# A decoder layer with 201 MB of expert weights: x and mem also come transposed, the norm's weights are applied at the split, and token tile 0 ends the projection and routes ahead of tile 1

## The chip, the cores and the metric

The kernel runs on one core of a Trainium2 chip. The metric is the device time of one execution in microseconds; the median of three runs stands for a kernel. A profile is one execution, recorded by the hardware.

## The reference

A decoder layer on 256 tokens of width 1024, all float32:

```
h   = rmsnorm(x) * attn_g ;  m = rmsnorm(mem) * mem_g
GLA (4 heads, chunks of 64, low-rank gate), MoBA (4 heads, causal softmax with ALiBi,
QK-norm), memory attention (4 heads into 256 memory tokens, QK-norm)  from  h @ w_in, m @ w_mem_kv
x2  = x + concat(heads) @ w_out
f   = rmsnorm(x2) * ffn_g
group = argmax(f @ w_rg + b_rg); two experts of the group's eight by f @ w_re + b_re
out = x2 + sum over the two of  p_group * p_e * ( silu(f @ w_gate[e]) * (f @ w_up[e]) ) @ w_down[e]
```

There are 32 experts of three 1024x512 matrices each, 201 MB in all. The kernel reads every expert's weights, whatever the routing.

## The kernel before

**Weights and their buffers.** All weights pass through SBUF in chunks of 1 MB, 128 partitions by 2048 floats. A pool `ring` has RING = 22 such buffers, and SyncE (SP) issues all loads in one order (line 106). First come 16 chunks of the attention part (`w_in`, `w_mem_kv`, `w_out`, packed by the host) and one buffer for mem; then 192 chunks of expert weights, 24 for each of 8 batches of four experts. In a batch, 16 chunks belong to gate and up (`w0g`, `w0u`) and 8 to down (`w0d`). Of every 25 expert chunks, the last three (LATE) lie in a pool that takes over the space of the attention part's scratch. Seven ring buffers hold no weights at first but scratch of the attention part: `hT` (two, the transposed x as a high and a low part), `memT` (two; later `mix`, the heads' output, which the output projection reads) and `sg0`, `sh0`, `sh1`. A load whose buffer is still in use waits on SP, and all loads behind it wait too. Expert chunks are numbered from 0 below: chunk 24 is the last for which there is room before the first expert chunk is used up; chunk 25 needs the buffer of a chunk that the gate product of batch 0 has read.

**Split products.** The projections are computed with two float32r parts per operand: `hi` is a rounded copy and `lo` the rest; `mm` runs three products, hi·hi, lo·hi and hi·lo (PASSES). `w(name, n)` splits one 128x512 piece of a weight chunk: ScalarE makes hi, VectorE makes lo. Before, `w` also multiplies each piece by the norm's weight (`gain`), and `x_T` and `mem_T` transpose x and mem on TensorE in pieces, which ScalarE and VectorE then split into hi and lo. hi has three buffers, lo two. The norm's weights come as rows in 14 small loads; `gains_T` turns them into columns.

**Order.** Inside the attention part every engine runs a list written out by hand (`order`), and `InOrder` keeps each engine to it. In the list `mb` (MoBA's q, k), `qk`, `e` (values of MoBA and mem's q), `kv`, `v`, `r` and `o` are projections; `gate_*`, `decayed` and `states` belong to GLA. The projection by `w_out` (`o`) runs both token tiles side by side, piece by piece, and its halves are added to `x2` (`add`). Then `row_T` transposes x2, `logits` and `bias` make router logits, `choose` picks groups and experts, `place` and `hot` make positions and a one-hot matrix, and `gather0` collects the tokens of the first four experts by products with it. After that the expert batches run (`batch`); gate and up first, then down.

Of the kernel before, what the change touches and what calls it, by code (L numbers as in the profile page):

```python
# [73 lines left out]
def layer(tc, x, mem, attn_norm_g, mem_norm_g, w_in, w_gla_gk, b_gla_gk, gla_out_norm_g,  # L74
          moba_q_norm_g, moba_k_norm_g, w_mem_kv, mem_q_norm_g, mem_k_norm_g, w_out,
          ffn_norm_g, w_router_group, b_router_group, w_router_expert, b_router_expert,
          w_gate, w_up, w_down, attn_pack, moe_pack, out):
    nc = tc.nc
    with ExitStack() as ctx:
        const = ctx.enter_context(tc.tile_pool(name="const", bufs=1))  # L80
        keep = ctx.enter_context(tc.tile_pool(name="keep", bufs=1))
# [45 lines left out]
        for s in [m[:, 0, 0:2] for m in hT + memT]:
            pool.memset(s.bitcast(F32), 0.0)

        win = w_in[0].rearrange("(i p) e -> p i e", p=P)  # L130

        def load_mem(t):
            r = mem_slot[0][:, D * t:D * t + D]
            load(out=r, in_=mem[0, P * t:P * t + P])
            return r


        gain_rows = [sg0[0:8, 1024:1152], sg0[32:47, 1024:1152]]
        gain_cols = fconst.tile([P, 24], F32, name="gain_cols")
        gfn = fconst.tile([P, KD], F32, name="gfn")  # L140
        g_attn, g_mem = (gain_cols[:, 8 * n:8 * n + 8] for n in range(2))
        g_qk, gno, bgk = gain_cols[:, 16:20], gain_cols[:, 20:21], gain_cols[:, 21:23]

        chunks = {}

        def load_chunk(name, h):

            chunks[name, h] = chunk(attn_pack[ATTN_CHUNKS.index((name, h))], f"w_{name}{h}", (4, 512))
# [15 lines left out]
        def load_small(what):  # L164
            rows = gain_rows[1]
            if what == "attn":
                load(out=gain_rows[0], in_=attn_norm_g[0].rearrange("(i p) -> i p", p=P))
            elif what == "mem":
                mem_slot.append(slot("mem"))
                mems.update((t, load_mem(t)) for t in range(NT))  # L170
            elif what == "mem gain":
                load(out=rows[0:8], in_=mem_norm_g[0].rearrange("(i p) -> i p", p=P))
            elif what == "ffn":
                load(out=g_ffn, in_=ffn_norm_g[0].rearrange("(p i) -> p i", i=KD))
                load(out=gfn.rearrange("p (q j) -> p q j", q=2), in_=ffn_norm_g[0].rearrange("(q p j) -> p q j", q=2, j=4))
            elif what == "qk gains":

                for n, g in enumerate((moba_q_norm_g, moba_k_norm_g, mem_q_norm_g, mem_k_norm_g)):
                    for half in range(2):
                        load(out=rows[8 + n:9 + n, 64 * half:64 * half + 64], in_=g[0:1])  # L180
            elif what == "gla":
                load(out=rows[12:13], in_=gla_out_norm_g[0:1])
                load(out=rows[13:15], in_=b_gla_gk[0].rearrange("(n p) -> n p", p=P))
            elif what == "lr":
                load(out=wlr, in_=win[:, :, 1536:1552])
            elif what == "gk":
                for p0 in (0, 32):
                    load(out=wgk[p0:p0 + 16], in_=w_gla_gk[0])
            elif what == "router":
                for q in range(2):  # L190
                    load(out=wr[:, 0, 4 * q:4 * q + 4, 0:4],
                         in_=w_router_group[0].rearrange("(q p j) g -> q p j g", q=2, j=4)[q])
                    load(out=wr[:, 1:5, 4 * q:4 * q + 4].rearrange("p g j e -> p g (j e)"),
                         in_=w_router_expert[0].rearrange("g (q p j) e -> q p g (j e)", q=2, j=4)[q])
                load(out=br[:, 0:4], in_=b_router_group[0:1, :].broadcast_to([P, 4]))
                load(out=br[:, 8:40], in_=b_router_expert.rearrange("l g e -> l (g e)").broadcast_to([P, 32]))

        loads = [
            (load_x, 0), (load_x, 1), (load_small, "attn"), (load_chunk, "mb", 0), (load_small, "mem gain"),
            (load_small, "lr"), (load_chunk, "mb", 1), (load_chunk, "qk", 0), (load_small, "qk gains"),  # L200
            (load_small, "mem"), (load_small, "gk"), (load_chunk, "e", 0), (load_small, "gla"), (load_chunk, "qk", 1),
            (load_chunk, "o", 0), (load_chunk, "e", 1), (load_chunk, "v", 0), (load_chunk, "kv", 1),
            (load_chunk, "r", 0), (load_chunk, "kv", 0), (load_chunk, "v", 1), (load_chunk, "r", 1),
            (load_small, "ffn"), (load_chunk, "o", 2), (load_chunk, "o", 3), (load_chunk, "o", 1),
            (load_small, "router"),
# [150 lines left out]
        def more_constants():  # L356
            state["iota_s"] = iota(const.tile([P, C], F32, name="iota_s"), [[1, C]], base=1)
            state["iota_e"] = iota(const.tile([P, NE], F32, name="iota_e"), [[1, NE]])
            state["iota_g"] = iota(const.tile([P, NE], F32, name="iota_g"), [[1, 4], [0, 8]])
# [5 lines left out]
            state["ones"] = const.tile([P, P], BF16, name="ones")
            pool.memset(state["ones"], 1.0)
            pool.memset(wr[:, 0, :, 4:8], 0.0)
            pool.memset(br[:, 4:8], -BIG)
            pool.memset(cur, 0.0)
# [11 lines left out]
        def w(name, n):  # L381

            src = chunks[name, n // 4][:, n % 4]
            hi, lo = weights[name, n] = [stage.tile([P, 512], F32R, name=f"{name}{n}_{part}", tag=part, bufs=bufs)
                                         for part, bufs in (("hi", 3), ("lo", 2))]
            if name == "o":
                split(src, hi, lo)
            else:
                gain = (g_mem if name == "kv" else g_attn)[:, n:n + 1]
                act.activation(hi, src, AF.Copy, scale=gain)  # L390
                dve.scalar_tensor_tensor(lo, src, gain, hi.bitcast(F32), op0=ALU.mult, op1=ALU.subtract)
# [80 lines left out]
        def x_T(t, q):  # L472
            norm_T(x2[:, t], t, q, hT, f"x{t}")
# [4 lines left out]
        def mem_T(t, q):  # L478
            norm_T(mems[t], t, q, memT, f"m{t}")

        def gains_T(n):
            rows = gain_rows[n]
            p0, k = 32 * n, rows.shape[0]
            pt = bank("tr", f"pt_gain{n}")[:, 0:k]
            pe.transpose(pt, rows, ident[p0:p0 + k, p0:p0 + k])
            act.copy(gain_cols[:, 8 * n:8 * n + k], pt)
# [40 lines left out]
        def lr_split():  # L527
            dve.tensor_tensor(wlr, wlr, g_attn.unsqueeze(2).to_broadcast([P, KD, 16]), op=ALU.mult)
# [655 lines left out]
```

## Time and profile before

| what | value |
|---|---|
| runs | 576.14, 575.94, 577.19 us; median 576.14 |
| profiled execution | 576.38 us, span 574.8 us, granted clock 0.964 |
| TensorE matmul busy | 482.8 us, 84% of the span |
| VectorE, ScalarE, GpSimd busy | 144.3, 111.1, 32.3 us |
| moved by DMA | 222.02 MB, 386 GB/s over the span |
| chain that ended last | DMA 64%, PE 28%, issue 4% |

The page cuts the span into 40 slices of 14.4 us and gives busy shares in tenths. A chain of waits follows the work that ended last back from the end, at each step to what released it. In timelines a row gives the start in us, the duration in us, the engine, the line, the operation, destination and source tiles, and how many instructions were merged. A float32 product shows as two records, a float32r product or a transpose as one. All operations that go through `InOrder` carry line 68.

### The profile page before, as it was taken

To read this page: it belongs to the slowest core of one execution; us is meant where nothing else is said; L and a number is where in the kernel's file an instruction comes from. 1 tells how busy PE (TensorE), PEld (TensorE's weight loads), DVE (VectorE), ACT (ScalarE), POOL (GpSimd) and SP (SyncE) were. 2 spreads that over 40 slices of the span, in tenths; PEclk is the share of its full clock that TensorE was granted. 3 is DMA by queue.
4 is the path that set the end of the run, shared out by engine and by line. 5 is a ranking of instruction groups with operands and counts; after the bars stand their busy time and mean duration, and the time that the engine had idled before them with its cause. 6 is when DMAs were issued, how large, how long until landed. Compare 5 with 4: busy or idle time off the path is not lost.

```text
span 574.8 us, 6813 instructions
## 1 busy us (share of the span) xinstructions
PE 482.8 (84%) x2695; PEld 244.3 (43%) x2695; DVE 144.3 (25%) x316; ACT 111.1 (19%) x217; POOL 32.3 (6%) x72
## 2 busy tenths in 40 slices
PE   5999999999989989777868976698669866996767
PEld 4896777788526226122412521252116211621113
DVE  2769877866306302000100000001000100020002
ACT  5676577642100010000000000001000100010000
POOL 1322230101000000000000000000000000000000
PEclk9999999999998999889997999999889989998899
DMA  8898946698999999999999999999999999999995
GB/s 297 352 421 285 417 151 225 229 391 306 392 421 420 420 423 419 421 421 422 418 421 421 422 418 422 424 418 421 423 422 418 423 421 422 418 423 422 420 421 197
DMA packets 35401, 222.02 MB, mean 386 GB/s; under 512 B 7411, under 2 KB 7974, under 8 KB 8742
## 3 DMA queue, kind: packets, MB, share of 16 engines
q1 hardware_dynamic: 34934, 221.02, 94.1%
q8 instruction: 22, 0.36, 0.3%
q10 hardware_dynamic: 432, 0.52, 0.2%
q14 instruction: 13, 0.11, 0.0%
HBM read 220.49 MB, written 1.05 MB: 385 GB/s over the span
## 4 chain that ended last, share of the span: by engine, by line
DMA 64%; PE 28%; issue 4%; DVE 2%; ACT 1%; POOL 1%; SPq 0%; ACTq 0%; DVEq 0%; POOLq 0%
DMA w4u<-in_moe_pack_dram 7%; DMA w3u<-in_moe_pack_dram 7%; DMA w7u<-in_moe_pack_dram 7%; DMA w6u<-in_moe_pack_dram 7%; DMA w5u<-in_moe_pack_dram 7%; DMA w2u<-in_moe_pack_dram 7%; DMA w4d<-in_moe_pack_dram 4%; DMA w7d<-in_moe_pack_dram 3%; DMA w2d<-in_moe_pack_dram 3%; DMA w6d<-in_moe_pack_dram 3%; DMA w5d<-in_moe_pack_dram 3%; DMA w3d<-in_moe_pack_dram 3%; PE pgate L979 2%; PE p_mb L68 2%; PE pup L979 2%
## 5 line engine op out<-in xcount | busy, mean ns | idle before, releaser
L884 PEld LDWEIGHTS pg_b<-ohs_b,x 128*128 128x128 f32 x224 | 55.3, 334 | 11.5 <-issue 10.1
L894 DVE TENSOR_TENSOR sg_b<-sg_b,pup 128x512 f32<-128x512 f32 x8 | 5.5, 688 | 217.3 <-PE pup L979 217.3
L884 PE MATMUL pg_b<-ohs_b,x 128*128 128x128 f32 x224 | 57.3, 407 | 1.9 <-DVE ohs_b L878 1.1
L893 ACT ACTIVATE sg_b<-pgate 128x512 f32<-128x512 f32 x8 | 4.8, 597 | 187.4 <-PE pgate L979 187.4
L887 DVE TENSOR_TENSOR xg_b<-pg_b,g_ffn 128x512 f32<-128x512 f32 x14 | 9.3, 688 | 111.8 <-PE pdn L992 77.5
L918 PE MATMUL acc<-y_b,sT_b 128*128 128x512 f32 x56 | 27.6, 615 | 4.2 <-ACT y_b L916 4.2
L916 ACT COPY y_b<-pdn 128x512 f32<-128x512 f32 x14 | 8.2, 585 | 113.5 <-PE pdn L992 98.1
L941 POOL TENSOR_TENSOR oh<-oh,gates 128x256 f32<-128x256 f32 x8 | 4.9, 616 | 311.1 <-DVE ohs_b L878 301.1
L68 PE MATMUL p_o<-o_hi,memT 128*128 128x512 f32 x64 | 20.6, 403 | 0.0
L979 PE MATMUL pup<-w5u,xg_b 128*32 128x512 f32 x64 | 14.9, 752 | 6.7 <-DMA w5u<-in_moe_pack_dram 6.7
L979 PE MATMUL pup<-w7u,xg_b 128*32 128x512 f32 x64 | 14.7, 738 | 6.9 <-DMA w7u<-in_moe_pack_dram 6.9
L979 PE MATMUL pgate<-w6g,xg_b 128*32 128x512 f32 x64 | 13.9, 753 | 6.0 <-DMA w6g<-in_moe_pack_dram 6.0
L979 PE MATMUL pgate<-w4g,xg_b 128*32 128x512 f32 x64 | 12.3, 673 | 6.9 <-DMA w4g<-in_moe_pack_dram 6.9
L918 PEld LDWEIGHTS acc<-y_b,sT_b 128*128 128x128 f32 x56 | 9.5, 190 | 18.7 <-ACT y_b L916 12.0
L979 PE MATMUL pup<-w6u,xg_b 128*32 128x512 f32 x64 | 12.9, 637 | 4.5 <-DMA w6u<-in_moe_pack_dram 4.5
L979 PE MATMUL pup<-w2u,xg_b 128*32 128x512 f32 x64 | 12.9, 758 | 4.0 <-DMA w2u<-in_moe_pack_dram 4.0
L979 PE MATMUL pup<-w4u,xg_b 128*32 128x512 f32 x64 | 11.8, 619 | 4.9 <-DMA w4u<-in_moe_pack_dram 4.9
L979 PE MATMUL pup<-w3u,xg_b 128*32 128x512 f32 x64 | 11.2, 612 | 5.3 <-DMA w3u<-in_moe_pack_dram 5.3
L68 PE MATMUL pdn<-w7d,hT_b 128*32 128x256 f32 (+1 forms) x96 | 12.4, 453 | 3.6 <-DMA w7d<-in_moe_pack_dram 2.9
L979 PE MATMUL pgate<-w3g,xg_b 128*32 128x512 f32 x64 | 11.7, 682 | 4.0 <-DMA w3g<-in_moe_pack_dram 4.0
L979 PE MATMUL pgate<-w7g,xg_b 128*32 128x512 f32 x64 | 12.0, 639 | 3.6 <-DMA w7g<-in_moe_pack_dram 3.6
L979 PE MATMUL pgate<-w5g,xg_b 128*32 128x512 f32 x64 | 11.9, 636 | 3.7 <-DMA w5g<-in_moe_pack_dram 3.7
(321 smaller groups left out, 759.2 us busy)
## 6 DMA issues: line engine op xcount, KB each, us to landing
w0g<-in_moe_pack_dram SPq DMA_DIRECT2D x8, 1024.0 KB
w0u<-in_moe_pack_dram SPq DMA_DIRECT2D x8, 1024.0 KB
w0d<-in_moe_pack_dram SPq DMA_DIRECT2D x8, 1024.0 KB
w1g<-in_moe_pack_dram SPq DMA_DIRECT2D x8, 1024.0 KB
w1u<-in_moe_pack_dram SPq DMA_DIRECT2D x8, 1024.0 KB
w1d<-in_moe_pack_dram SPq DMA_DIRECT2D x8, 1024.0 KB
w2g<-in_moe_pack_dram SPq DMA_DIRECT2D x8, 1024.0 KB
w2u<-in_moe_pack_dram SPq DMA_DIRECT2D x8, 1024.0 KB
```

What stands on the lines that cost most here:

```text
L68: r = getattr(self.engine, name)(*args, **kwargs)
L884: nc.tensor.matmul(pgs[q][:, j], x2_i[:, t, 4 * q + j], ohs[:, t], start=(t == 0 and j == 0), stop=(t == NT - 1), skip_group_check=True)
L887: nc.vector.tensor_tensor(xg[:, 4 * q:4 * q + 4], pgs[q], g_ffn[:, 4 * q:4 * q + 4].unsqueeze(2).to_broadcast([P, 4, P]), op=ALU.mult)
L893: nc.scalar.activation(sg, pg, AF.Silu)
L894: nc.vector.tensor_tensor(sg, sg, pu, op=ALU.mult)
L916: nc.scalar.copy(y, pdn)
L918: nc.tensor.matmul(acc[t][half], sT[:, P * t:P * t + P], y, start=first, stop=last, skip_group_check=True)
L941: nc.gpsimd.tensor_tensor(oh, oh, gates[:, :, EB * b:EB * b + EB].unsqueeze(3).to_broadcast([P, NT, EB, C]), op=ALU.mult)
L979: nc.tensor.matmul(ps[s], xg[:, i, s], tiles[(b, kind, c, e // 2)][:, e % 2, ii], start=(i == 0), stop=(i == KD - 1))
```

## The change

- The host also passes x and mem transposed (`t_pack`, loaded in halves of 512 KB to `raw`); the plain x and mem are still loaded. `x_T`, `mem_T` and `gains_T` go. `x_split(k)` and `mem_split(k)` make hi and lo of one 128x256 piece, eight for each, and multiply it by the norm's weight there; `w` only splits. The small inputs come packed in four loads.
- `warm_up` runs 13 products of zeros before the first data is there; `keep_warm` goes. `x_norm` and `mem_norm` move behind the first products that use the transposed data. lo gets three buffers.
- The ring now also holds two `raw` buffers, and `w4` splits a whole chunk of `w_out` into two ring buffers, twice (four buffers).
- At the end of the projection, tile 0's products come before tile 1's, and tile 0's add, norm, logits, choice and positions are put between tile 1's products. `gather0` is cut by token tile: the part of tile 0 comes ahead of `place(1)`.

```diff
-        hT = [slot(f"hT{n}", F32R).rearrange(...) for n in range(2)]
+        raw = [slot(f"raw{n}").rearrange("p (a b) -> p a b", a=KD) for n in range(2)]
+        hT, memT = [[slot(f"{name}{a}", F32R) for a in range(2)] for name in ("hT", "memT")]
...
         loads = [
-            (load_x, 0), (load_x, 1), (load_small, "attn"), (load_chunk, "mb", 0), (load_small, "mem gain"),
-            (load_small, "lr"), (load_chunk, "mb", 1), (load_chunk, "qk", 0), (load_small, "qk gains"),
...
+            (load, gains, gain_pack), (load_T, 0, 0), (load_chunk, "mb", 0, 0), (load_chunk, "mb", 0, 1), (load_T, 0, 1),
+            (load_chunk, "mb", 1), (load, sh1[:, 0:128], lr_pack), (load_chunk, "qk", 0), (load_x, 0), (load_x, 1),
+            (load_chunk, "qk", 1), (load, wgk, gk_pack), (load_chunk, "e", 0), (load_chunk, "e", 1), (load_T, 1, 0),
+            (load_T, 1, 1), (load_mem,), (load_chunk, "kv", 0), (load_chunk, "kv", 1), (load_chunk, "v", 0),
...
+        def T_split(n, k):
+            src, (hi, lo), gain = raw[n][:, k], ((hT, memT)[n][a][:, k] for a in range(2)), (g_attn, g_mem)[n][:, k:k + 1]
+            act.activation(hi, src, AF.Copy, scale=gain)
+            dve.scalar_tensor_tensor(lo, src, gain, hi.bitcast(F32), op0=ALU.mult, op1=ALU.subtract)
...
+        def w4(name, n):
+            parts = [slot(f"{name}{n}_{v}", F32R).rearrange("p (a b) -> p a b", a=4) for v in ("hi", "lo")]
+            for m in range(4):
+                split(chunks[name, n // 4][:, m], *(v[:, m] for v in parts))
+                weights[name, n + m] = [v[:, m] for v in parts]
...
+        def warm_up(n):
+            ps = bank("tr", "warm_up")
+            for _ in range(n):
+                pe.matmul(ps, zeros[:, 0:P], zeros[:, 0:512], start=True, stop=True)
...
+            (w, "o", 15), (mm, "o", 14, 1), (mm, "o", 14, 0), (w4, "o", 0), (mm, "o", 7, 1), (mm, "o", 7, 0),
+            (w4, "o", 8), (mm, "o", 15, 0), (mm, "o", 15, 1), (mm, "o", 0, 0), (mm, "o", 1, 0), (mm, "o", 2, 0),
+            (mm, "o", 3, 0), (add, 0, 0), (mm, "o", 8, 0), (square, 0, 0), (mm, "o", 9, 0), (row_T, 0, 0, 0),
+            (mm, "o", 10, 0), (mm, "o", 11, 0), (add, 0, 1), (mm, "o", 0, 1), (square, 0, 1), (logits, 0, 0),
+            (mm, "o", 1, 1), (rstd, 0), (row_T, 0, 1, 0), (mm, "o", 2, 1), (mm, "o", 3, 1), (add, 1, 0),
+            (logits, 0, 1), (square, 1, 0), (bias, 0), (mm, "o", 8, 1), (c, 0, 3), (mm, "o", 9, 1), (row_T, 1, 0, 0),
+            (c, 0, 3), (mm, "o", 10, 1), (mm, "o", 11, 1), (logits, 1, 0), (add, 1, 1), (c, 0, 3), (square, 1, 1),
+            (row_T, 1, 1, 0), (place, 0), (logits, 1, 1), (rstd, 1), (h, 0, 3), (bias, 1), (gather0, 0, 0, 4),
+            (c, 1, 9), (gather0, 0, 4, 4), (place, 1), (h, 1, 3), (gather0, 1, 0, 2), (gathered0, 0, 2),
+            (gather0, 1, 2, 2), (gathered0, 2, 2),
```

## Rows read from the trace of the kernel before

**Rows 1.** The page, 40 slices: busy tenths of the DMA engines, and GB/s.
```profile
DMA  8898946698999999999999999999999999999995
GB/s 297 352 421 285 417 151 225 229 391 306 392 421 420 420 423 419 421 421 422 418 421 421 422 418 422 424 418 421 423 422 418 423 421 422 418 423 422 420 421 197
```
**Rows 2.** Windows: busy us (instructions) by engine, clock, DMA share, GB/s.
```profile
0.00:150.00 150.00, 142.57 (x807) 113.09 (x808) 104.23 (x238) 89.13 (x177) 27.95 (x65) 1.00 0.81 309
150.00:560.00 410.00, 329.72 (x1817) 126.17 (x1819) 37.00 (x72) 20.60 (x38) 4.31 (x7) 0.95 1.01 421
40.00:50.00 10.00, 9.99 (x59) 7.78 (x58) 8.23 (x11) 8.13 (x13) 2.54 (x2) 1.00 1.02 409
50.00:60.00 10.00, 8.98 (x46) 6.78 (x45) 9.36 (x20) 5.91 (x11) 2.30 (x2) 1.00 0.78 226
```
**Rows 3.** The chain of waits in order of time: start us, us, what.
```profile
32.54 0.44 PE pt_m L68 x4
51.89 0.60 DVE sg L68
52.49 1.39 DVE e_lo L68
58.00 8.47 PE p_kv L68 x36
197.66 19.79 DMA w2u<-in_moe_pack_dram
537.28 19.83 DMA w7d<-in_moe_pack_dram
557.15 4.50 PE pdn L68 x40
```
**Rows 4.** Timeline of SP's issues: chunks 15, 21, 22 and 25.
```profile
116.62 0.33 SPq L106 DMA_DIRECT2D w0u<-in_moe_pack_dram  x1
132.73 0.33 SPq L106 DMA_DIRECT2D w0d<-in_moe_pack_dram  x1
137.81 0.33 SPq L106 DMA_DIRECT2D w0d<-in_moe_pack_dram  x1
146.48 0.33 SPq L106 DMA_DIRECT2D w1g<-in_moe_pack_dram  x1
```
**Rows 5.** Windows of the first loads, columns as in Rows 2.
```profile
2.00:3.00 1.00, 0.00 (x0) 0.00 (x0) 0.00 (x0) 0.20 (x1) 0.55 (x3) 1.00 0.93 332
```
**Rows 6.** Timeline of TensorE: first products, end of the projection, routing, first gate product.
```profile
10.30 1.22 PE L68 MATMUL p_mb<-mb_hi,hT 128*128 128x512 f32 x2 [0.59 <-ACT mb_hi L68]
14.31 1.05 PE L68 MATMUL p_mb<-mb_hi,hT 128*128 128x512 f32 x2
16.19 0.62 PE L68 MATMUL p_mb<-mb_hi,hT 128*128 128x512 f32 x2
24.19 0.40 PE L68 MATMUL p_qk<-hT,qk_hi 128*128 128x256 f32 x2
132.53 0.98 PE L68 MATMUL pl<-wr,xT 128*128 128x40 f32 x8
140.51 4.05 PE L68 MATMUL pg_b<-ohs,x 128*128 128x128 f32 x16
144.53 1.92 PE L979 MATMUL pgate<-w0g,xg_b 128*32 128x512 f32 x16
```
**Rows 7.** Timeline of ScalarE: splits of 512 and work of 256 columns.
```profile
5.37 0.58 ACT L65 CAST hT<-pt_x 128x512 fp32r<-128x512 f32 x1 [3.16 <-PE pt_x L68]
9.53 1.34 ACT L68 ACTIVATE mb_hi<-w_mb,gain_cols 128x512 fp32r<-128x512 f32 x2 [1.72 <-DMA w_mb<-in_attn_pack_dram]
55.56 0.46 ACT L68 ACTIVATE sh<-p_e,r_x 128x256 f32<-128x256 f32 x1
```
**Rows 8.** Timeline of VectorE: the same.
```profile
5.99 0.69 DVE L65 TENSOR_TENSOR hT<-pt_x,hT 128x512 fp32r<-128x512 f32 x1 [5.99 <-ACT hT L65]
59.25 0.48 DVE L68 SCALAR_TENSOR_TENSOR qn_mq<-p_e,r_x,rs_mq 128x256 f32<-128x256 f32 x1 [0.54 <-POOL rs_mq L68]
```

More of the change, by code (lines that the diff above doesn't have):

```diff
@@ L32 @@
 BIG = 1e30
+HI = 3
 RING = 22
@@ L111, in chunk @@
             return v
+        zeros = work.tile([P, 512], F32, name="zeros", tag="w2").bitcast(BF16)
+        dve.memset(zeros, 0.0)
         ident = const.tile([P, P], F32, name="ident")
@@ L126, in layer @@
             pool.memset(s[:, 0:1], 0.0)
[L127 to L148, printed above, removed]
+        gains = const.tile([P, 40], F32, name="gains")
+        g_attn, g_mem, g_ffn, gfn = (gains[:, n:n + 8] for n in (0, 8, 24, 32))
+        g_qk, gno, bgk = gains[:, 16:20], gains[:, 20:21], gains[:, 21:23]
@@ L159, in layer, with load_chunk @@
-        mems, mem_slot = {}, []
+        chunks, mems = {}, {}
+        def load_chunk(name, h, part=None):
+            src = attn_pack[ATTN_CHUNKS.index((name, h))]
+            if part is None:
+                chunks[name, h] = chunk(src, f"w_{name}{h}", (4, 512))
+                return
+            if part == 0:
+                chunks[name, h] = slot(f"w_{name}{h}").rearrange("p (a b) -> p a b", a=4)
+            load(out=chunks[name, h][:, 2 * part:2 * part + 2],
+                 in_=src.rearrange("p (a b) -> p a b", a=4)[:, 2 * part:2 * part + 2])
@@ L161, in load_x, with load_T @@
+        def load_T(n, q):
+            load(out=raw[n][:, 4 * q:4 * q + 4], in_=t_pack[n, q].rearrange("p (a b) -> p a b", a=4))
         def load_x(t):
             load(out=x2[:, t], in_=x[0, P * t:P * t + P])
[L164 to L196, printed above, removed]
@@ L198, in layer, with load_mem @@
-        loads = [
-            (load_x, 0), (load_x, 1), (load_small, "attn"), (load_chunk, "mb", 0), (load_small, "mem gain"),
-            (load_small, "lr"), (load_chunk, "mb", 1), (load_chunk, "qk", 0), (load_small, "qk gains"),
[L201 to L205, printed above, removed]
+        def load_mem():
+            m = slot("mem").rearrange("p (a b) -> p a b", a=NT)
+            for t in range(NT):
+                mems[t] = m[:, t]
+                load(out=mems[t], in_=mem[0, P * t:P * t + P])
@@ L381, in w @@
         def w(name, n):
[L383 to L391, printed above, removed]
+            hi, lo = (stage.tile([P, 512], F32R, name=f"{name}{n}_{v}", tag=v, bufs=HI) for v in ("hi", "lo"))
+            split(chunks[name, n // 4][:, n % 4], hi, lo)
+            weights[name, n] = hi, lo
+        def w4(name, n):
[3 more added lines that the diff above has]
+                weights[name, n + m] = [v[:, m] for v in parts]
         def sums(name, n):
@@ L470, in x_norm, with x_split, mem_split @@
             norm(x2[:, t], r_x[:, t:t + 1], f"x{t}")
-        def x_T(t, q):
-            norm_T(x2[:, t], t, q, hT, f"x{t}")
+        def x_split(k):
+            T_split(0, k)
         def mem_norm(t):
             norm(mems[t], r_mem[:, t:t + 1], f"m{t}")
[L478 to L486, printed above, removed]
+        def mem_split(k):
+            T_split(1, k)
         def rx_T(part):
@@ L789, in layer @@
         sel = sm_tile([P, NT, NE], "sel", BF16)
-        pps = [bank("at", f"pp{t}")[:, 0:32] for t in range(NT)]
+        pps, pgs0 = {}, {}
         oh0 = oh_pool.tile([P, NT, EB, C], F32, name="oh0", tag="oh")
         ohs0 = oh_pool.tile([P, NT, EB, C], F32, name="ohs0", tag="ohs", bufs=1)
-        xg0 = keep.tile([P, KD, P], F32, name="xg_b0", tag="xg")
         def choose(t):
@@ L826, in gather0, with gathered0, c @@
+        def gathered0(i0, n):
+            dve.tensor_tensor(state["xg0"][:, i0:i0 + n], pgs0[i0 // 4][:, i0 % 4:i0 % 4 + n],
                               g_ffn[:, i0:i0 + n].unsqueeze(2).to_broadcast([P, n, P]), op=ALU.mult)
-        def keep_warm(n):
-            ps = bank("mm", "warm")[:, 0:256]
+        choosing = [choose(t) for t in range(NT)]
+        placing = [hot(t) for t in range(NT)]
+        def c(t, n=1):
             for _ in range(n):
-                pe.matmul(ps, ident, x2[:, 0, 0:256], start=True, stop=True)
@@ L834, in layer, with h @@
-        c0, c1 = (choose(t) for t in range(NT))
-        h0, h1 = (hot(t) for t in range(NT))
-        def steps(*parts):
-            for p in parts:
-                next(p)
-        steps(*[c0] * 3)
-        bias(1)
-        steps(*[c0, c1] * 6)
-        keep_warm(4)
-        place(0)
-        steps(c1, h0, c1, h0, c1, h0)
-        keep_warm(2)
-        place(1)
-        steps(h1, h1, h1)
-        gather0(0, 2)
-        gather0(2, 2)
+                next(choosing[t])
+        def h(t, n=1):
+            for _ in range(n):
+                next(placing[t])
@@ L853, in layer @@
+        for f, *args in order:
+            f(*args)
+        iota_s, iota_e, iota_g, ltri, ones = (state[k] for k in ("iota_s", "iota_e", "iota_g", "ltri", "ones"))
+        fctx.close()
+        ex = ctx.enter_context(tc.tile_pool(name="ex", bufs=2))
+        late = ctx.enter_context(tc.tile_pool(name="late", bufs=LATE))
         ng = sm_tile([P, NT, 2], "ng")
```

205 lines of the change are left out of this document (102 added, 103 removed).

## The prediction

> **What bounds the kernel now.** I read the page's slices first. From about 150 us on the DMA engines never rest: nine tenths in every slice, 418 to 424 GB/s [rows 1]. The window from 150 to 560 us confirms it, 421 GB/s at a share of 1.01, while before 150 us the share is 0.81 [rows 2]. The chain of waits then shows what late time consists of: from 197.66 us it runs from landing to landing, eight chunks in 19.8 us, 2.48 us per chunk of 1 MB, up to 557.1, and only then does TensorE's last work follow [rows 3]. So behind some moment the time is chunks times 2.48 us plus a fixed end, and nothing that TensorE gains there counts. What counts is when that unbroken stream begins.
>
> The timeline of SP's issues gives that moment. Chunk 22 goes out at 137.81, and chunk 25 only at 146.48 [rows 4], when the first gate product (144.53, sixteen records in 1.9 us) has released a buffer [rows 6]. All 25 buffers were full by then; the queue was empty. So before, the stream begins at 146.48, and TensorE's progress sets it. In front of that the DMA engines idled 0.19 x 150 = 28 us for want of free buffers, and TensorE was dense: 142.6 us busy of 150 [rows 2].
>
> **The change part by part.** I call S the number of us by which the projection phase on TensorE comes earlier.
>
> *Start, 5.9 us gained.* Before, the first split product starts at 10.30, after x (1 MB), a 1 MB chunk, transposes and splits; the last of the 48 `mb` products ends by 24.19 [rows 6]. After, x's first half and half a chunk, 1.07 MB, suffice. From 2.0 us at 332 GB/s [rows 5] that is 5.2, with 0.8 us until a wait sees it 6.0; one split of 0.67 (half of the pair at 9.53) [rows 7] gives 6.7. Before, twelve products starting at 10.30 take 4.9 us, 0.41 each: the pair at 14.31 is 1.05 long, that at 16.19 only 0.62, and later ones come every 0.23 us (36 in 8.47) [rows 3, 6]. [...] I take it that the 13 products of zeros, at 0.41 each 5.3 us from about 1.5, bring the rise forward; if not, 12 x 0.2 = 2.4 us are lost again. So 48 x 0.23 = 11.0, plus 0.6 of waiting for the first low halves: 18.3 against 24.19.
>
> *Transposes, 1.3 us gained.* After 24.19 three `mem_T` of 0.44 us go [rows 3].
>
> *A stall, up to 2.0 us gained.* At 51.89 TensorE waits 2.0 us for VectorE, for `decayed` and a low half behind it [rows 3]. With three low buffers VectorE may run ahead. Dense, TensorE would be 5.9 + 1.3 + 2.0 = 9.2 us earlier: the upper bound of S.
>
> *What the splits cost, 2.9 us lost.* They lie in VectorE's fullest stretch. From 40 to 60 us it is busy 8.23 + 9.36 = 17.6 us [rows 2]. Two `mem_T` parts of 0.69 go, eight `mem_split` parts come; the nearest row of 256 columns is 0.48 [rows 8]: 17.6 - 1.4 + 3.8 = 20.0. TensorE could do its own work there in 20 - 0.9 (transposes) - 2.0 (stall) = 17.1. VectorE is then the bound, 2.9 us longer. Between no loss and this I take the full 2.9, since VectorE runs a fixed list and cannot reorder. S = 9.2 - 2.9 = 6.3. ScalarE gets 8 x 0.46 - 2 x 0.58 = 2.5 us more there [rows 7], plus `mem_norm`, on 14.0 busy of 20 [rows 2]: hidden.
>
> The same piece of work tells how the change of shape is priced. Eight of 256 columns cost 8 x 0.48 = 3.8 against 4 x 0.69 = 2.8 us of VectorE per input, 8 x 0.46 = 3.7 against 4 x 0.58 = 2.3 of ScalarE [rows 7, 8]. [...]
>
> *`x_norm` moved behind `qk`'s first products.* `mb_norm` waits for it and `w("qk", 3)` is queued behind both on ScalarE. I price it at nothing, since `mem_norm`, as long, leaves the same stretch; without that cover it is one to two us of S.
>
> *More bytes, nothing.* 2.1 MB more are 5.0 us of DMA at 421 GB/s [rows 2]. They lie before 55 us, ahead of 28 us of DMA idleness. If the cover went, 5.0 us would be paid. The 14 small loads, and SP's waits around them, go at the same place: no effect for the same reason, and all attention chunks come before their use.
>
> *The end of the projection.* Before, tile 1's last product ends at 132.5 [rows 6]. Now two `logits` of 0.98 and a `row_T` of 0.44 stand ahead of it: 132.5 + 2.6 - S. Behind it: `logits` (0.98), `row_T` (0.44) and its copy, `logits`, then gathering tile 0, eight float32 products. Sixteen records, eight products, take 4.05 us [rows 6], so this is 4.05; `place(1)` is queued behind it on TensorE, though it needs none of it. Then one-hot work and two products: about 10.3 us in all. The first gate product starts at 135.1 - 6.3 + 10.3 = 139.1 instead of 144.53.
>
> *Who is late next: the loads.* Before, 24 ring buffers were asked for ahead of chunk 0. Now it is 26 (two `raw` more) and four by `w4`. The two `raw` come back early, so chunk k waits for a release four places later: chunk 11, not 15, gets `sh1`, free at 116.62 before [rows 4]. In my count SP never waits long from there on: 11 to 25 are 15 chunks, each 2.48 us. Chunk 25 is served as if issued 14 x 2.48 = 34.7 after 116.62 - S, at 151.3 - S, against 146.48: a gain of S - 4.9. If `w4` takes buffers only when it runs, four chunks come earlier; but chunk 19 needs `mix` or a `w4` buffer, free at the projection's end (as chunk 21 got `mix` at 132.73 before [rows 4]), so at 135.1 - S, and six chunks on that is 150.0 - S: a gain of S - 3.6 at most. With S = 6.3 these are 1.4 and 2.7; I take 2.0. The gate's 5.4 us are therefore mostly not passed on, because chunk 25 is no longer released by the gate but waits in the queue.
>
> The sum: 576.38 (span 574.8 and 1.6 around it) - 2.0 = 574.4. That execution was 0.24 above the median, so against 576.14 I say 574.3.
>
> **Rivals.** *TensorE keeps everything.* VectorE keeps pace, S = 9.2: gain 4.3 to 5.6, about 571.2. For it: VectorE idles 2.4 us of 40 to 60 and gets a buffer more. Against it: 20.0 us of work for a stretch of 17.1.
>
> *The gain ends at the buffers or is not made.* S is 4 to 5: products of zeros don't raise the clock (S = 3.9), or `x_norm` adds two us. Then -0.3 to +1.0: 576.2. For it: the stream's condition takes 3.6 to 4.9 us of any S.
>
> *Slower: `w4` is served ahead of the loads.* If buffers are given in the program's order, and `w4`'s only when ScalarE reaches it, SP holds chunk 0 until then, two us of splits behind `sh1`'s release: 116.6 + 2.0 - 6.3 = 112.3. Then 25 chunks begin there: chunk 25 is served at 112.3 + 25 x 2.48 = 174.3, against 146.48: 28 us more, 604. It decides at the first expert load: later than 100 us or not. Against it: before, chunks were issued as attention buffers came free.
>
> **How the numbers follow.** Forecast (573.0 to 575.5) 0.50; everything kept 0.15; no gain (575.5 to 577.6, a tenth of it faster) 0.30; `w4` ahead 0.05. A measurement of this kernel tells 0.2% from nothing, 1.15 us: faster is below 575.0. Of the forecast 0.44 lies there, with 0.15 and 0.03: faster 0.62. Same 0.23: 0.06 of the forecast, 0.17 of no gain. Slower 0.15: 0.10 of no gain, and 0.05. The range goes from S = 9.2 with the later bound, 570.6, to S = 3.9 with the earlier, 577.4.
>
> **What would show it.** Right: `mb` ends near 18.3; TensorE waits for VectorE's low halves before `kv`; the gate product starts near 139; SP's issues from chunk 15 on come ahead of the landings by a queue, and chunk 25's buffer is free before its turn. Wrong: DMA idle after 125 us, the first 12 products still 0.41 apart, or a first expert load after 100 us.

## The result, and the profile after

The changed kernel takes 580.66 us (median; 579.87 to 582.46) against 576.14 beside it: ratio 1.0082, 95% interval 1.0057 to 1.0107. It is slower by 4.5 us where 1.8 less were forecast, and above the forecast's upper end of 577.4. The profiled execution has a span of 579.1 us, before 574.8.

The page's slices of the changed kernel, DMA engines and GB/s: nine tenths in every slice from about 116 us on, where before it was from about 144 us on [rows 1]. The stream begins earlier and still ends later.

```profile
DMA  8999537499999999999999999999999999999995
GB/s 296 405 421 386 195 134 278 178 418 407 422 416 420 420 418 419 419 418 420 420 420 421 418 422 417 423 418 418 420 419 421 419 421 418 422 418 421 419 419 200
```

Windows of the changed kernel, columns as in [rows 2]: the first five answer to [rows 2, 5], two more are places where the stream is not full, and in the last the first gate product runs.

```profile
0.00:150.00 150.00, 141.83 (x780) 108.14 (x780) 101.82 (x245) 86.15 (x184) 28.62 (x62) 0.98 0.80 316
150.00:560.00 410.00, 319.44 (x1783) 122.69 (x1780) 37.12 (x72) 21.20 (x38) 4.32 (x7) 0.97 1.01 419
40.00:50.00 10.00, 8.84 (x46) 6.30 (x45) 9.64 (x16) 7.89 (x15) 2.99 (x2) 1.00 1.00 413
50.00:60.00 10.00, 9.08 (x41) 6.65 (x42) 6.58 (x20) 7.99 (x21) 5.29 (x6) 1.00 0.90 348
2.00:3.00 1.00, 1.00 (x4) 0.39 (x3) 0.00 (x0) 0.00 (x0) 0.94 (x3) 1.00 0.57 127
114.00:115.00 1.00, 1.00 (x6) 0.82 (x5) 0.45 (x2) 1.00 (x3) 0.00 (x0) 1.00 0.38 148
130.00:132.00 2.00, 2.00 (x12) 1.72 (x11) 0.68 (x5) 0.59 (x1) 0.00 (x0) 1.00 0.96 336
144.00:146.00 2.00, 2.00 (x12) 0.39 (x8) 0.84 (x6) 1.09 (x6) 0.00 (x0) 0.50 0.99 410
```

The stream moves 419 GB/s and not 421, and VectorE is busy 9.64 of the ten us from 40 to 50, where it was 8.23. From 40 to 60 it is busy 16.2 us in all, not the forecast 20.0: three of the eight `mem_split` parts start before 40.

The chain of waits of the changed kernel: start us, us, what; the stage after `kv`, and rows that answer to the end of [rows 3].

```profile
63.82 1.09 PE pa L69 x16
200.83 19.88 DMA w2u<-in_moe_pack_dram
541.50 19.89 DMA w7d<-in_moe_pack_dram
561.43 4.50 PE pdn L69 x40
```

The last landing in the chain (chunk 187; the other four are not waited for in it) is at 541.50 + 19.89 = 561.39; before it was 557.11 [rows 3]. These 4.28 us are the whole loss of the profiled execution. At the chunk where both chains can be laid side by side (200.83 and 197.66) it is already 3.17; the other 1.1 come later, for a step over eight chunks, pauses aside, takes 19.87 to 19.90 us and not 19.79 to 19.83.

SP's issues of chunks 11 and 25 in the changed kernel, against chunks 15 and 25 of [rows 4].

```profile
113.87 0.33 SPq L106 DMA_DIRECT2D w0u<-in_moe_pack_dram  x1
147.11 0.33 SPq L106 DMA_DIRECT2D w1g<-in_moe_pack_dram  x1
```

Chunk 11 now gets the release that chunk 15 got: the shift by four is as forecast. But that release (`sh1`) comes at 113.87 against 116.62. So S is 2.75 us, and not 6.3. The stage after `kv` shows the same, 63.82 against 66.69 in the chain of the kernel before:

```profile
66.69 1.09 PE pa L68 x16
```

TensorE in the changed kernel: first product, last of `mb`, first of `qk`, three waits, the logits behind the projection, first gate product [rows 6].

```profile
8.46 0.71 PE L69 MATMUL p_mb<-mb_hi,hT 128*128 128x512 f32 x2 [1.32 <-ACT mb_hi L69]
19.70 0.39 PE L69 MATMUL p_mb<-mb_lo,hT 128*128 128x512 f32 x1
19.93 0.40 PE L69 MATMUL p_qk<-hT,qk_hi 128*128 128x256 f32 x2
25.27 0.39 PE L69 MATMUL p_qk<-hT,qk_lo 128*128 128x256 f32 x1 [0.70 <-DVE qk_lo L69]
49.85 0.50 PE L69 MATMUL p_e<-e_lo,hT 128*128 128x512 f32 x1 [0.99 <-DVE e_lo L69]
57.88 0.50 PE L69 MATMUL p_kv<-kv_lo,memT 128*128 128x512 f32 x1 [0.92 <-DVE kv_lo L69]
132.12 0.98 PE L69 MATMUL pl<-wrb,xT 128*128 128x40 f32 x8
143.65 3.42 PE L939 MATMUL pgate<-w0g,xg_b 128*32 128x512 f32 x16
```

All three waits are for low halves, which VectorE writes. The gate product starts 0.9 us earlier, not 5.4, and ends later, for it takes 3.42 us and not 1.92: the granted clock was 0.50 there (from 144 to 146 us). With the old end it takes 1.92 or 1.93 in the runs below.

ScalarE at the start: the first split waits for `raw`, then for its table, then the weights' half lands. The last row is the first of `x_norm`'s two squares.

```profile
4.86 1.28 ACT L66 ACT_TABLE_LOAD   x1 [4.86 <-DMA raw<-in_t_pack_dram]
6.15 0.51 ACT L66 ACTIVATE hT<-raw,gains 128x256 fp32r<-128x256 f32 x1
7.70 0.62 ACT L69 CAST mb_hi<-w_mb 128x512 fp32r<-128x512 f32 x1 [1.04 <-DMA w_mb<-in_attn_pack_dram]
20.42 1.05 ACT L69 ACTIVATE junk_x<-x 128x1024 bf16<-128x1024 f32 x1
```

VectorE in the changed kernel: a split of `mem` between others in `e`, and a wait for GpSimd that holds `kv_lo` back.

```profile
49.72 0.47 DVE L69 SCALAR_TENSOR_TENSOR memT<-raw,gains,memT 128x256 fp32r<-128x256 f32 x1
56.69 0.48 DVE L69 SCALAR_TENSOR_TENSOR qn_mq<-p_e,r_x,rs_mq 128x256 f32<-128x256 f32 x1 [2.38 <-POOL rs_mq L69]
```

### The profile page after: what moved, and what is told of

Its sections match the earlier page's. It is cut to its first block, busy times and chain, and to the rows that moved or that the text cites. A ratio compares the mean times of both kernels' runs of the same rounds, so it can differ in the third digit from the quotient of the medians.

```text
span 579.1 us, 6693 instructions
## 1 busy us (share of the span) xinstructions
PE 474.7 (82%) x2662; PEld 236.9 (41%) x2662; DVE 142.0 (25%) x323; ACT 108.7 (19%) x224; POOL 32.9 (6%) x69
## 3 DMA queue, kind: packets, MB, share of 16 engines
HBM read 222.62 MB, written 1.05 MB: 386 GB/s over the span
## 4 chain that ended last, share of the span: by engine, by line
DMA 76%; PE 19%; DVE 2%; ACT 1%; POOL 1%; issue 1%; SPq 0%; DVEq 0%; POOLq 0%; ACTq 0%
DMA w4u<-in_moe_pack_dram 7%; DMA w3u<-in_moe_pack_dram 7%; DMA w5u<-in_moe_pack_dram 7%; DMA w6u<-in_moe_pack_dram 7%; DMA w2u<-in_moe_pack_dram 7%; DMA w7u<-in_moe_pack_dram 7%; PE p_o L69 4%; DMA w6d<-in_moe_pack_dram 3%; DMA w5d<-in_moe_pack_dram 3%; DMA w7d<-in_moe_pack_dram 3%; DMA w1d<-in_moe_pack_dram 3%; DMA w1u<-in_moe_pack_dram 3%; DMA w3d<-in_moe_pack_dram 3%; DMA w2d<-in_moe_pack_dram 3%; DMA w4d<-in_moe_pack_dram 3%; DMA w_r<-in_attn_pack_dram 3%
## 5 line engine op out<-in xcount | busy, mean ns | idle before, releaser
L844 PEld LDWEIGHTS pg_b<-ohs_b,x 128*128 128x128 f32 x224 | 55.3, 334 | 11.7 <-issue 10.3
L847 DVE TENSOR_TENSOR xg_b<-pg_b,gains 128x512 f32<-128x512 f32 x14 | 9.3, 688 | 110.6 <-PE pdn L953 74.7
L939 PE MATMUL pup<-w4u,xg_b 128*32 128x512 f32 x64 | 13.1, 685 | 6.1 <-DMA w4u<-in_moe_pack_dram 6.1
L939 PE MATMUL pup<-w3u,xg_b 128*32 128x512 f32 x64 | 12.5, 685 | 6.1 <-DMA w3u<-in_moe_pack_dram 6.1
L939 PE MATMUL pup<-w7u,xg_b 128*32 128x512 f32 x64 | 11.6, 600 | 6.1 <-DMA w7u<-in_moe_pack_dram 6.1
L939 PE MATMUL pup<-w5u,xg_b 128*32 128x512 f32 x64 | 11.9, 611 | 5.1 <-DMA w5u<-in_moe_pack_dram 5.1
L939 PE MATMUL pgate<-w7g,xg_b 128*32 128x512 f32 x64 | 10.8, 600 | 6.1 <-DMA w7g<-in_moe_pack_dram 6.1
L939 PE MATMUL pgate<-w6g,xg_b 128*32 128x512 f32 x64 | 10.8, 600 | 6.1 <-DMA w6g<-in_moe_pack_dram 6.1
L939 PE MATMUL pgate<-w4g,xg_b 128*32 128x512 f32 x64 | 10.8, 600 | 6.1 <-DMA w4g<-in_moe_pack_dram 6.1
L953 PE MATMUL pdn<-w2d,hT_b 128*32 128x512 f32 x64 | 10.8, 601 | 5.8 <-DMA w2d<-in_moe_pack_dram 5.8
L939 PE MATMUL pup<-w1u,xg_b 128*32 128x512 f32 x64 | 11.6, 689 | 2.7 <-DVE tmp L1028 2.7
```

The source lines that it names most:

```text
L844: nc.tensor.matmul(pgs[q][:, j], x2_i[:, t, 4 * q + j], ohs[:, t], start=(t == 0 and j == 0), stop=(t == NT - 1), skip_group_check=True)
L847: nc.vector.tensor_tensor(xg[:, 4 * q:4 * q + 4], pgs[q], g_ffn[:, 4 * q:4 * q + 4].unsqueeze(2).to_broadcast([P, 4, P]), op=ALU.mult)
L939: nc.tensor.matmul(ps[s], xg[:, i, s], tiles[(b, kind, c, e // 2)][:, e % 2, ii], start=(i == 0), stop=(i == KD - 1))
L953: nc.tensor.matmul(pdn[half][s], hT2[:, c, s], tiles[(b, "d", c, e // 2)][:, e % 2, 512 * half:512 * half + 512], start=(c == 0), stop=(c ...
```

## The experiments

My theory after this reading: the four buffers of `w4` cost 4.9 us of stream, S gives back only 2.75 since VectorE has no room, and something slows the stream itself. Rivals: the new front as such costs; the gate product still sets the stream. A time below is a median; "before" was 576.3 to 576.7 beside these runs.

### Where the gain went: four runs

**Front alone.** The changed front, with the end of the kernel before.

```diff
-(w4,"o",0) ... (w4,"o",8) ... tile 0's logits, choosing, placing, gathering, then tile 1's
+(w,"o",0) ... both tiles side by side; then steps(...), place, gather0 as before
```

> The changed front (transposed inputs from the host, gains at the split, zeros ahead, third low buffer) with the end of the kernel before: no w4, the two token tiles side by side, routing and gathering in the old order. Theory (queue): the four w4 buffers moved chunk 25's release four places back, so that the stream hangs on the release of sh1 and not on the gate product; without them the stream begins at the gate product again, which comes earlier by what the front gains, 2.8 us: 576.1 - 2.8 = 573.3, and SP issues chunk 25 near 143.7. Rival (front): the 2.1 MB more and the new tensors are what costs, the stream's pace is lower by them: 578 or more, and chunk 15 is again issued at sh1's release. If the slower pace of the changed kernel's stream (19.95 against 19.87 us per eight chunks, 1.3 us over all) belongs to the front, 574.6.

Measured: 576.17 us, ratio 0.9995 (0.998 to 1.001). Neither number. Its SP timeline and its chain of waits:

```profile
115.39 0.33 SPq L106 DMA_DIRECT2D w0u<-in_moe_pack_dram  x1
145.28 0.33 SPq L106 DMA_DIRECT2D w1g<-in_moe_pack_dram  x1
```

```profile
398.77 19.88 DMA w5u<-in_moe_pack_dram
```

Without `w4` it is chunk 15 again that gets `sh1`, and chunk 25 goes out ahead of 146.48 [rows 4] with the gate product: the loss of 4.5 us goes away with `w4`. The step stays at 19.88, so the slower pace belongs to the front, which makes 574.6 of the expected 573.3. The other 1.6 us are not explained. The profiled execution, at 579.27 the slowest of twelve, began at the lower clock (its window from 9 to 12 us, columns as in [rows 2], clock 0.50); whether the other eleven did is not on record.

```profile
9.00:12.00 3.00, 3.00 (x8) 2.16 (x7) 2.99 (x7) 2.76 (x6) 0.00 (x0) 0.50 1.01 419
```

**End alone.** The kernel before with `w4`, the new order behind it and its pools.

> The kernel before with the changed end alone: w4 in four ring buffers, tile 0 projected, routed and gathered ahead of tile 1. Theory (queue): S is 0 here, and the shift costs its full price, 4.9 us of stream and up to 1 us for the stretch behind sh1's release in which the stream is not yet full: 576.1 + 4.9 to 5.9 = 581.0 to 582.0; chunk 11 is issued when chunk 15 was (116.6), although the gate product comes earlier than at 144.5. Rival (front): the end as such is free, its earlier gate product keeps its gain: 576 or less.

Measured: 582.85 us, ratio 1.0114 (1.009 to 1.0138): 6.5 us slower, a little over the upper end. Chunk 11 gets `sh1`; the step is the old one.

```profile
115.92 0.33 SPq L108 DMA_DIRECT2D w0u<-in_moe_pack_dram  x1
```

```profile
395.27 19.81 DMA w5g<-in_moe_pack_dram
```

**A later gate product,** in the changed kernel and in the one before.

```diff
+for _ in range(7): pe.matmul(ps, ident, x2[:, 0, 0:256], ...)   # ahead of place(1)
```

> The changed kernel with seven products of ident and x2 (256 columns, float32, some 3 us) put on TensorE ahead of place(1), so that the first gate product comes 3 us later. Theory (queue): chunk 25's buffer is released about 6 us ahead of its turn, so the time is the same within 0.5 us: 580.7. Rival (gate): the first gate product's release still sets when the stream begins: 583.7.

> The kernel before with seven more products in its keep_warm ahead of place(1), some 3 us. Both theories: here the gate product's release sets the stream, so all of it shows: 579.1, and SP issues chunk 25 near 149.5. If it shows less than 2 us, the reading of the kernel before was wrong: its stream does not hang on the gate product.

Measured: 581.45 (ratio 1.0092, 1.0071 to 1.0113) and 579.03 (1.005, 1.0033 to 1.0068). SP's issue of chunk 25, first in the changed kernel with the delay, then in the one before with it:

```profile
150.56 0.33 SPq L106 DMA_DIRECT2D w1g<-in_moe_pack_dram  x1
```

```profile
149.00 0.33 SPq L106 DMA_DIRECT2D w1g<-in_moe_pack_dram  x1
```

Before, 2.5 us later at the issue gives 2.7 in the time: the gate sets the stream. After, 3.45 us later give 0.8 in the median: it does not. But the spare time was 2 to 3 us and not 6, for with the delay the stream does run dry, as two windows of that kernel show (GB/s last). From issue to landing is longer than a share of the stream: the first two expert chunks of the changed kernel, issued at 54.99 and 58.99, landed after 5.3 and 4.8 us, where a share is 2.48. By an estimate from these, chunk 25 has to be issued the difference, 2.3 to 2.8 us, ahead of its turn to keep the stream whole. The two windows:

```profile
150.00:152.00 2.00, 2.00 (x14) 0.44 (x6) 1.41 (x7) 0.00 (x0) 0.62 (x1) 0.82 0.62 176
152.00:154.00 2.00, 2.00 (x10) 0.66 (x10) 0.43 (x1) 1.12 (x2) 0.00 (x0) 1.00 0.85 340
```

### What slows the stream: five runs

**Old places of the inputs in memory.**

```diff
+for name in _OLD: held[name] = nc.dram_tensor(...)   # all 22 inputs, in the old order
```

> The changed kernel with every input of the kernel before declared again in its old place and order (those not used are never read), so that the packed expert weights lie in memory where they lay before; the instructions are the same. In the runs so far the step between two landings eight chunks apart is 19.88 to 19.90 us in all three kernels with the changed front and 19.79 to 19.82 in all three with the old one, whatever the end. Theory (place in DRAM): the step falls to 19.81, and over the 165 chunks from chunk 23 on, 20.6 steps, the time falls by 20.6 x 0.08 = 1.7 us: 579.0. Rival (something else of the front, as the address of the ring in SBUF, 128 bytes further on): the step stays at 19.89, time 580.7.

Measured: 581.57, ratio 1.0087 (1.0071 to 1.0103). That theory falls, the chain of waits has the same step:

```profile
381.41 19.89 DMA w5u<-in_moe_pack_dram
```

**Start of the ring buffers in SBUF.** The new `gains` tile is 128 bytes longer than the `g_ffn` it replaced and lies ahead of the ring.

```diff
-gains = const.tile([P, 40], ...)
+gains = fconst.tile([P, 40], ...);  g_ffn = const.tile([P, KD], ...)
```

> The changed kernel with the tile gains in the pool that is freed after the projection, and only the eight columns that live on in the constants, as before. So the 22 ring buffers start at byte 19360 of a partition, 416 over a multiple of 512, as in all three kernels with the step of 19.81 (15264 and 19360); in all that showed 19.89 they start at 19488, 32 over. Old places of the inputs in memory did not change the step. Theory (address of the buffers): the step falls to 19.81 and the time by 20.6 x 0.08 = 1.7: 579.0. Rival (nothing of the address): 19.89 and 580.7.

Measured: 579.69, ratio 1.0061 (1.0038 to 1.0084). The chain of waits:

```profile
380.18 19.80 DMA w5u<-in_moe_pack_dram
```

The step is back, and the chain's last landing comes 1.66 us earlier (559.73). The 128 bytes are the cause of the slower step. In the median 1.0 us of the 1.7 shows, and the intervals of the two ratios overlap.

**Ring on a multiple of 512 bytes,** in the version with early norms (below) and in the kernel before; and 256 over.

```diff
+pre = tile_pool("pre")    # iota_s, iota_e, iota_g: 384 bytes (or iota_s alone: 128)
+ring = tile_pool("ring")  # then const, keep, ...
```

> The kernel with the norms early and the old end (575.5), its ring allocated first, behind 384 bytes of constants, so that each buffer starts at a multiple of 512 bytes. Theory (address): a buffer of 8192 bytes that starts on the boundary is served at least as fast as one at 416: step 19.81 or less, time 575.5 - 1.7 = 573.8 or less. Rival: the step stays 19.89 and the time 575.5.

> The kernel before, only its ring allocated first behind 384 bytes of constants (start 1536, a multiple of 512, against 15264). Theory (place alone): the step falls from 19.81 to about 19.55, and the time by 20.6 x 0.26 = 5.4: 570.7. Rival (the place matters only with the changed front): 576.1.

> The same with the ring behind 128 bytes of constants: start 1280, 256 over a multiple of 512. If what counts is the boundary of 512 bytes, the step stays at 19.8 or more (576); if a boundary of 256 does, it is 19.55 as on the multiple (570.7). If the low end of SBUF is what counts, it is 19.55 here too; the step of the kernel before with the ring at 15264 and of the end alone at 19360 were the same, which speaks against that.

Measured: 569.09 (ratio 0.9861, 0.9843 to 0.9879), where the same kernel had 575.47 with its ring 32 over; 571.79 (0.9915, 0.9901 to 0.9928); 572.23 (0.992, 0.9908 to 0.9933). A step of each from the chain of waits, in that order:

```profile
414.08 19.55 DMA w5d<-in_moe_pack_dram
```

```profile
434.89 19.58 DMA w6u<-in_moe_pack_dram
```

```profile
413.96 19.56 DMA w5d<-in_moe_pack_dram
```

So the place alone does it, without the changed front too, and 256 is as good as 512: about 19.56 us at 0 and 256, 19.81 at 416, 19.89 at 32. One rival is left by the edits: all three rings also begin at the low end of SBUF (1280 or 1536, against 15264 to 19488). The chain of the second speaks against it. Its ring begins 15264 - 1536 = 13728 bytes lower, less than two of its 22 buffers of 8192 bytes, and yet all its steps of eight chunks, two pauses aside, take 19.48 to 19.71 us, also those in which no buffer below the old start is filled.

### What held S down: five runs

**Norms early,** with the changed end, and with the old one.

```diff
-(mm,"qk",2,0), (x_norm,1), (mm,"qk",2,1), (x_norm,0) ... (mm,"kv",0,0), (mem_norm,0) ... (mem_norm,1)
+(w,"qk",2), (x_norm,1), (w,"qk",1), (x_norm,0), (w,"qk",0) ... (w,"qk",6), (mem_norm,0), (mem_norm,1)
```

> The changed kernel with three pieces of its order moved: x_norm of both tiles between the first qk weights, where ScalarE waits for TensorE anyway (17.7 to 19.9), both mem_norm behind the seventh qk weight (ScalarE idle 28.1 to 30.8), and mem loaded two loads earlier so that it is there. Theory: the waits at 24.2 to 25.3 (1.0 us, qk_lo behind x_norm) and at 56.9 and 60.3 (1.4 us, kv_lo behind mem_norm's chain over GpSimd) go; S grows from 2.75 to about 5.2, sh1 is released at 111.4, and as the queue starts there all of it reaches the end: 580.7 - 2.4 = 578.3. Rival (VectorE has no room): the gain in qk is eaten where VectorE is late in e, S grows by 1.4 at most and the time is 579.3 or more. Rival (gate): the time follows the gate product, not sh1's release.

> The changed front with the same three moves and the end of the kernel before (no w4). Theory: the stream starts at the gate product, which comes earlier by S: front alone gave 576.2, so 576.2 - 2.4 = 573.8. Rival (VectorE has no room): 574.8 or more.

Measured: 582.99 (ratio 1.0119, 1.0105 to 1.0134) and 575.47 (0.9989, 0.9975 to 1.0003): no gain beyond the noise in either, the rival's side. The first one's release of `sh1` and its wait in `e`:

```profile
113.81 0.33 SPq L106 DMA_DIRECT2D w0u<-in_moe_pack_dram  x1
```

```profile
51.16 0.50 PE L69 MATMUL p_e<-e_lo,hT 128*128 128x512 f32 x1 [1.72 <-DVE e_lo L69]
```

The waits in `qk` and `kv` are gone; the one in `e` grew from 0.99 to 1.72, and `sh1` came 0.06 us earlier; from the first `qk` product (20.25) to it are 93.56 us, in the changed kernel 93.94. In the second one's windows, VectorE (third number with a count) has not a gap:

```profile
44.00:48.00 4.00, 4.00 (x23) 2.89 (x21) 4.00 (x8) 3.25 (x7) 1.61 (x1) 1.00 1.01 412
48.00:52.00 4.00, 2.27 (x13) 1.58 (x12) 4.00 (x8) 1.17 (x3) 1.29 (x1) 1.00 1.02 414
```

Why the first is even slower than the changed kernel stays open. In the profiled execution TensorE's last work begins at 561.15, 0.28 us ahead of the changed kernel's 561.43, so the difference lies behind the stream: that work begins with 6.03 us where it was 4.50.

```profile
561.15 6.03 PE pdn L69 x40
```

**Without the low halves of `mem`** (left out of the computation; norms early, old end).

```diff
-dve.scalar_tensor_tensor(lo, src, gain, hi, ...)   # for mem only
```

> The kernel with the norms early and the old end (575.5), without the eight VectorE instructions that write the low halves of mem (they are zeros here, written once by GpSimd; the output is therefore less exact). Theory (VectorE has no room): it was 4.00 of 4.00 us busy from 44 to 52 and TensorE waited 1.7 us for e_lo at 50.9; with 8 x 0.48 = 3.8 us less that wait goes, S grows by 1.7 to 2.4 and the time falls to 573.1 to 573.8. Rival (the wait is ScalarE's or GpSimd's): S and the time stay.

Measured: 574.12, ratio 0.9954 (0.9938 to 0.997), 0.35% below the kernel with them by the two ratios. TensorE's wait in `e` is 0.35 us. The profiled execution began at the lower clock (0.65 from 9 to 12 us), its first `qk` product came at 21.74 against 19.99 with the low halves, and yet `sh1` was free at 113.60 against 113.58: the stretch between is 1.7 us shorter.

```profile
51.04 0.50 PE L69 MATMUL p_e<-e_lo,hT 128*128 128x512 f32 x1 [0.35 <-DVE e_lo L69]
```

**Splits of `mem` early,** nothing left out.

```diff
-(mem_split,0..7) between the splits of e;  loads: e1, T(1,0), T(1,1), mem
+(w,"qk",6), (mem_split,0..3) ... 4..7 where 0..3 were;  (w,"e",6), (mem_norm,0), (mem_norm,1);  loads: T(1,0), T(1,1), e1, mem
```

> Nothing left out: changed front and old end, x_norm early, mem's first four splits in VectorE's and ScalarE's idle time from 28 to 31 us (mem's transposed halves loaded ahead of the second e chunk), the other four where the first four were, both mem_norm behind the last e weight, and the ring's old address. Theory: VectorE has 1.9 us less in 44 to 52, and the waits in qk and kv go too: S grows from 2.8 to about 5, and the stream starts at the gate product: 575.5 - 2.0 - 1.7 (step 19.81) = 571.8. Rival (VectorE's work is only moved, and comes late elsewhere): 573.8.

Measured: 571.52, ratio 0.9909 (0.989 to 0.9928), as the theory says. The first gate product:

```profile
139.94 1.93 PE L949 MATMUL pgate<-w0g,xg_b 128*32 128x512 f32 x16
```

**Without the products of zeros.**

```diff
-(warm_up, 13),
```

> The changed kernel without the 13 products of zeros. The prediction's term: the first 12 products at 0.40 and not 0.23 us, 2.0 to 2.4 us of S lost at the end of mb. The starts at the lower clock seen in other runs cost 1.5 us of sh1's release (115.05 against 113.58), the rest being eaten by VectorE's stretch: 580.7 + 1.5 = 582.2. Rival (the zeros do nothing): 580.7.

Measured: 584.11, ratio 1.0136 (1.0122 to 1.0151), 3.4 us over the changed kernel and more than expected. In its TensorE timeline the pair that took 0.63 takes 1.05, and `mb` ends 2.2 us later:

```profile
10.04 1.05 PE L69 MATMUL p_mb<-mb_hi,hT 128*128 128x512 f32 x2
21.91 0.40 PE L69 MATMUL p_mb<-mb_lo,hT 128*128 128x512 f32 x1
```

`sh1` is released at 116.08 there, 2.2 us later as well: VectorE's stretch ate nothing of it. The other 1.2 us are not explained.

### All together: two runs

The first is norms early and old end with the old places in memory; the second is splits early with the ring at 1536. Both have

```diff
-(warm_up, 13)
+(warm_up, 20)
```

> The run before, with the old places of the inputs in memory as well and 20 products of zeros in place of 13, so that no gap lies between them and the first real product (in the profiled run of front alone the gap was 2.2 us and the first products came at 0.40 us each and not 0.23). Theory: 573.8 - 1.7 (the step back at 19.81) - about 0.6 (no run starts at the lower clock) = 571.5, and the runs scatter less. If the place in memory is not what slows the step: 573.2.

Measured: 575.59, ratio 0.9985 (0.9972 to 0.9998): a miss, since the memory layout did nothing (above) and 20 zeros for 13 did not move the median.

> The version with the splits early (571.5), its ring at a multiple of 512 bytes and 20 products of zeros in place of 13. The causes add: 571.5 - 20.6 x 0.26 (5.4) - about 0.6 (no start at the lower clock) = 565.5. If they don't add (the faster stream waits for TensorE): 568.

Measured: 566.27, ratio 0.9818 (0.9805 to 0.983): faster than both kernels, 0.8 us from the sum of the parts. Its release of `sh1`, its gate product and a step of its chain, one view each:

```profile
110.72 0.33 SPq L107 DMA_DIRECT2D w0u<-in_moe_pack_dram  x1
```

```profile
138.58 1.92 PE L948 MATMUL pgate<-w0g,xg_b 128*32 128x512 f32 x16
```

```profile
409.32 19.56 DMA w5d<-in_moe_pack_dram
```

S is 116.62 - 110.72 = 5.9 here, near the forecast 6.3, with the same front and its splits and norms in other places.

## Why the prediction was wrong, step by step

**Right: the mechanism.** The stream sets the time, chunk k takes the release of chunk k+4, and of the gate's lead nothing counts any more. Chunk 11's issue shows the shift, the late gate shows the rest, and the end alone is slower where the front alone is not. The first expert load came at 54.99 us, so `w4` was not served ahead of the loads. The 2.1 MB more cost nothing that any run shows. With the measured S the formula S - 4.9 is a loss of 2.15 us. The projection's end also came where its sum puts it with that S: 135.1 - 2.75 = 132.35, and the logits behind it start at 132.12. The gate product then came 1.0 us later than the 10.3 us of routing allow, and took 1.5 longer; neither counted.

**Wrong: the size of S,** a term of the sum: 2.75 and not 6.3. Its start and its stall were taken too large, and the moved norms, priced at nothing, cost time. Up to the end of `kv` the terms were

- the start 4.26 (first `qk` product at 19.93 against 24.19), not 5.9. The weights' half landed at 7.70 and not 6.0: the first loads moved 127 GB/s from 2 to 3 us, where I had taken the 332 of [rows 5]. Zeros were worth 2.2 of it, by the run without them; that they would bring the quicker pace forward was an assumption until then. No run shows the 0.8 us until a wait sees a landing, an estimate of mine: the half landed 5.8 us after its issue at 1.84, and its split began within 0.1 us;
- the stall in `e` 1.0, not 2.0. I took the length of VectorE's links in the chain [rows 3] for TensorE's idle time; the window says 10 - 8.98 = 1.02 [rows 2];
- the transposes 1.3, as forecast, if the three `mem_T` are taken at their 0.44;
- the waits for low halves 2.8 of idle time (0.70 in `qk`, 0.17 and 0.99 in `e`, 0.92 in `kv`), against 2.9. That these are so near is luck, for only the 1.2 in `e` has the forecast cause, a VectorE without room. In `qk` the low half comes late because `x_norm`'s two squares keep ScalarE from 20.42 to 22.5 and `mb_norm` stands behind them; in `kv` VectorE itself idles 2.38 us for GpSimd, where a part of `mem_norm` is ahead in the queue;
- a rest: 4.26 + 1.3 + 1.0 - 2.8 = 3.8, but the stage after `kv` starts 2.9 us earlier (63.82 against 66.69). Most of these 0.9 us lie in `kv`, whose products take 0.8 longer from start to start with no idle time on record; to which term they belong stays open.

So pricing `x_norm` and `mem_norm` at nothing was a slip: they stand in front of 1.6 of the 2.8. But moved away alone they gave 0.4 us from the first `qk` product to `sh1`, because VectorE's list in `e` was then late. Only fewer or earlier splits there moved S (without the low halves, and splits early).

Three small slips in the sums change nothing here: two `logits` and a `row_T` are 2.4 us and not 2.6, 150.0 - 146.48 is 3.5 and not 3.6, and 574.4 less 0.24 is 574.2 and not 574.3.

The splits of 256 columns, priced at 0.48 us each [rows 8], took VectorE 0.47 to 0.48 in the changed kernel, and two in a row 0.87 (from 46.06 on).

**Missed: the pace of the stream,** which no term had. 0.08 us per step over 20.6 steps are 1.7 us; the pauses in the two profiled runs were not equal, and 1.3 of it show in the last landing. It was the 128 bytes of `gains`.

**Left over: 0.8 us.** I had the stream unbroken behind `sh1`. It falls to 148 GB/s for a microsecond and at 130 to 336 for two, 1.0 us of transfer together. But before, too, it was not full at once (274 and 352 GB/s from 146 to 148 and 148 to 150), so how much of the 0.8 this is stays open. I also took 2.0 of the bounds 1.4 and 2.7, where the later turn was true.

Together: 3.55 (S) + 0.6 (the bound) + 1.3 + 0.8 = 6.3, against 580.7 - 574.4 = 6.3.

**The rivals.** "Ends at the buffers" had the mechanism, but with an S of 3.9 to 5 it stopped at +1.0, and it knew neither the pace nor the gaps. The slower rival (`w4` ahead) was not what made it slower; the queue that the forecast itself described was.

## What to carry to other kernels

Where a stream of equal chunks sets the time, count the buffers asked for ahead of it: one more moves every later chunk one release back, which here turned an earlier gate product into a loss (the end alone, with four more: 6.5 us slower). VectorE, whose list had no gap, was not relieved by moving what waited in front of it (0.4 us); take work out of such a stretch, into one with gaps. And look at where the stream's buffers start: a tile 128 bytes longer ahead of them changed the pace of all that followed, from 19.81 to 19.89 us per eight chunks.

## What the runs showed of the hardware

Buffers of 8192 bytes per partition that start at a multiple of 256 bytes of SBUF were filled faster in these runs: about 19.56 us per eight chunks at 0 and 256, against 19.81 at 160 and 19.89 at 32 over a multiple of 256; in the kernel before this alone is worth 0.85% (ratio 0.9915). Why the start counts, and why 32 over is slower than 160, no run shows.

With the 13 products of zeros the first pairs of `mb` products take 0.63 us in the changed kernel and not 1.05, as without them, but not in every execution: in the profiled runs of front alone, of ring on 512, of no low halves and of splits early the granted clock was 0.50 to 0.65 from 9 to 12 us, and in the last three of these the pairs behind the first take up to 1.05 again. With 20 of them, which end 0.7 us ahead of the first product or at it, the pairs behind the first take 0.63 in both profiled runs. The clock column alone does not tell: without zeros it says 1.00 from 7 to 20 us, where the first pairs take 1.05.
